# Attention scores from row slices of split features instead of stacked copies, and the mixed-feature loads in other slots of the weight region

## The chip, the cores and the metric

The kernel runs on one core of a Trainium2 chip. What counts is the device time of one execution in microseconds, as the median of several runs. All times are in microseconds unless ns stands beside them.

## What is computed

The reference is a backbone of two layers over 256 context tokens and 512 latent tokens, 1024 features wide, in float32. In each layer a modulated RMS norm and one input projection feed three mixers: differential attention (4 heads, each with two softmax components of 32 features), grouped-query attention (6 query heads, 2 key heads, 64 features) and a gated delta rule in both directions (6 heads, "GDN" below). Their outputs are joined, projected back and added; then follows a SwiGLU block. The last layer needs latent queries only. The two attention mixers, cut to what the change touches:

```
# differential attention
s = einsum('bqhcd,bkhcd->bhcqk', q, k) * scale        # two components c of 32 features each
p = softmax(s);  p = p[:, :, 0] - lam * p[:, :, 1]
o = einsum('bhqk,bkhe->bqhe', p, v)
# grouped-query attention
s = einsum('bqhgd,bkhd->bhgqk', q, k) * 64 ** -0.5
o = einsum('bhgqk,bkhd->bqhgd', softmax(s), v)
```

Latent queries read all 768 tokens, context queries the 256 context tokens.

## The kernel before, in words

Float32 products are made of float32r matmuls: a number x is split into hi, its rounding, and lo = x - hi, and a product becomes hi*hi + hi*lo + lo*hi (`mm3` and `split`, lines 222 to 233). Most of the time goes to the projections and the SwiGLU block, with features on the partitions and tokens on the free axis.

The change touches the mixers of each layer. `mixers` (line 972) runs a plan written out by hand (`PLAN`, line 38): its items `p` and `s` are the preparation and the twelve sequential steps of the GDN, `o` its output, `a` a piece of the attention. Program order and the given priorities go to a scheduler, which orders each engine's instructions by when it expects them to be ready; on the chip every engine then runs its own list in order.

The attention (`attention`, line 1268) goes over five pairs of heads in the order 2, 0, 3, 1, 4 (`HORD`). Pairs 0 and 1 are differential, 2 to 4 grouped-query. Within a pair it goes over query tiles of 128 tokens: four latent ones in both layers, two context ones in layer 0 besides. `ASTEP` says after which query tiles the next pair is prepared: `f` and `t` are the first and second part of `attn_prep` (line 1212), and `o` writes out the pair before.

`attn_prep` loads queries and keys with tokens on partitions, turns them on TensorE (tile `exp`) and splits them: `to_feat` (line 1092) leaves hi and lo with 128 features on the partitions, in slots of tag `f`. For a differential pair the 128 features are four components of 32 rows. For each component, `stack4` (line 1114) multiplies its 32 rows of hi and of lo by a constant 0/1 matrix `pick`, which is loaded by `pick_setup`, so that 128 rows hold (hi, hi, lo, lo) for queries and (hi, lo, hi, lo) for keys. The products stand in PSUM tile `stk` and are copied to SBUF tiles `qs` and `ks` (tag `t`): by VectorE where the columns are context, by ScalarE where they are latent. One matmul over 128 rows then gives all products of a score. `stack2` (line 1129) does the like for grouped-query pairs by copying halves of 64 partitions (`gqs`, `gks`); two matmuls give a score.

`scores` (line 1165) fills one PSUM tile `S` of two banks (768 columns as two halves of 384) for one softmax component. There are two such tiles, s0 and s1, taken in turn. `softmax` (line 1155) takes the maximum on VectorE (`nm`, line 1161) and the exponential on ScalarE (`P`, L182 in the rows). `attend` (line 1174) combines the two components of a differential head on VectorE, turns P on TensorE (`pt`, `PT`), and multiplies by V (`pv`). The PSUM tiles m0 and m1 are a ring (line 146) that `exp`, `stk`, `pt`, `pv` and `otr` share.

Last in the plan is `mixed` (line 958): it closes the GDN's memory and opens the weight region W of three raw slots, four hi slots and four lo slots (line 1422), loads seven of the eight mixed feature tiles from DRAM (`mx`, into the raw slots, on SyncE's queue) and splits them into `mhi` and `mlo`. The output projection `outproj` (line 1313) then loads the weights `w_o` through the same raw slots, on ScalarE's queue, and splits them (`whi`, `wlo`). Line 188 is the helper that issues every matmul of `mm`, 191 every transpose on TensorE, 185 every copy on ScalarE, 161 every two-operand VectorE or GpSimd operation, 182 every activation. In the rows TensorE is PE and its weight loads PEld, VectorE DVE, ScalarE ACT, GpSimd POOL. In a matmul's shape, as 32*128, the first number is the rows of the array that it uses.

Of the kernel before, what the change touches and what calls it, by code (L numbers as in the profile page):

```python
# [10 lines left out]
F32 = mybir.dt.float32  # L11
# [11 lines left out]
NT = TOK // 128  # L23
# [44 lines left out]
ATTN = (dict(t=10, f=4, p=4, q=3, v=2, d=2, w=2, g=4, u=1),  # L68
        dict(t=10, f=3, p=4, q=4, v=2, d=2, w=2, g=4, u=1))
# [25 lines left out]
class Net:  # L95
# [862 lines left out]
    def mixed(self, l, side, parts):  # L958
# [7 lines left out]
        for kt in self.early_k(l):  # L966
            x = self.W.slot("mx", F32, "raw")
            self.dma(x[:, t0:TOK], self.mixd[kt][:, t0:TOK])
            for a, n, _ in parts:
                self.split(self.at(self.mhi, kt, a, n), self.at(self.mlo, kt, a, n), x[:, a:a + n])  # L970
# [121 lines left out]
    def to_feat(self, src, t0, name):  # L1092

        hi, lo = (self.slot(name, F32R, tag="f") for _ in range(2))
# [7 lines left out]

    def pick_setup(self):

        self.pick = self.R.tiny("pick", [128, 4, 128], F32R)
        raw = self.slot("pickraw", tag="d")[:, :512]
        self.dma(raw, self.A["pick"])
        self.cp(self.pick.rearrange("p a b -> p (a b)"), raw)

    def parts_of(self, t0):  # L1110

        return ((t0, 2), (2, NT)) if t0 < 2 else ((2, NT),)

    def stack4(self, feat, c, kind, t0, name):

        x = self.slot(name, F32R, tag="t")
        r = slice(32 * c, 32 * c + 32)
        for a, b in self.parts_of(t0):
            ps = self.ring("stk")[:, :128 * (b - a)]
            w = slice(128 * a, 128 * b)  # L1120
            for hl in range(2):
                self.mm(ps, self.pick[r, 2 * kind + hl], feat[hl][r, w], hl == 0, hl == 1)
            if a < 2:
                self.v.tensor_copy(x[:, w], ps)
            else:
                self.cp(x[:, w], ps)
        return x

    def stack2(self, src, t0, name, k):


        out = [[self.slot(name, F32R, tag="g" if k else "t") for _ in range(2 if k else 1)] for _ in range(2)]
        for a, b in self.parts_of(t0):
            ps = self.ring("exp")
            w = slice(128 * a, 128 * b)
            for i in range(a, b):
                self.tr(ps[:, 128 * (i - a):128 * (i - a) + 128], src[:, i])
            for c in range(2):
                own, other = slice(64 * c, 64 * c + 64), slice(64 - 64 * c, 128 - 64 * c)
                p = ps[own, :128 * (b - a)]  # L1140
                hi, lo = out[c][0], out[c][-1]
                self.cp(hi[own, w], p)
                if k:
                    self.cp(hi[other, w], p)
                    self.sub(lo[own, w], p, hi[own, w].bitcast(F32))
                self.sub(lo[other, w], p, hi[own, w].bitcast(F32))
        return out
# [17 lines left out]
    def scores(self, pairs, qt, nk):  # L1165
        ps = self.big("S")
        halves = 2 if nk == 768 else 1
        w = nk // halves
        for hf in range(halves):
            for i, (qT, kT) in enumerate(pairs):  # L1170
                self.mm(ps[:, hf, :w], qT[:, 128 * qt:128 * qt + 128], kT[:, hf * w:hf * w + w], i == 0, i == len(pairs) - 1)
        return ps if nk == 768 else ps[:, 0, :nk]

    def attend(self, l, pair, O, qts):

        for qt in qts:
# [4 lines left out]
            for hd, (comps, V) in enumerate(pair):  # L1181
                Ps = [self.softmax(self.scores(pr, qt, nk), nk, Z[:, hd, ci:ci + 1]) for ci, pr in enumerate(comps)]
                P = Ps[0]
                if len(comps) == 2:
# [5 lines left out]
                for i, k0 in enumerate(range(0, nk, 384)):  # L1190
# [4 lines left out]
                    if i < EVD[l][len(comps) - 1]:  # L1195
# [7 lines left out]
            for kb in range(nkb):  # L1203
                for c in range(2):
                    self.mm(pv[64 * c:64 * c + 64, :128], pair[c][1][:, kb], PTs[c][:, 128 * kb:128 * kb + 128], kb == 0, kb == nkb - 1)
# [6 lines left out]
    def attn_prep(self, l, i):  # L1212


        t0 = 2 if l == DEPTH - 1 else 0
        if i < 2:
            q = self.load_tok(self.dqk[:, :, 128 * i:128 * i + 128], t0, "dq")
            k = self.load_tok(self.dqk[:, :, 256 + 128 * i:256 + 128 * i + 128], 0, "dk")
            q = self.to_feat(q, t0, "qT")
            yield  # L1220
            q = [self.stack4(q, c, 0, t0, "qs") for c in range(4)]
            k = self.to_feat(k, 0, "kT")
            comps = [[(q[c], self.stack4(k, c, 1, 0, "ks"))] for c in range(4)]
            vs = self.load_tok(self.dkv[:, :, 256 + 128 * i:256 + 128 * i + 128], 0, "vs", "v")
            yield [(comps[2 * c:2 * c + 2], vs[:, :, 64 * c:64 * c + 64]) for c in range(2)]
# [6 lines left out]
        q2 = self.stack2(q, t0, "gqs", False)  # L1232
        yield [([[(q2[c][0], k) for k in self.gks[c]]], self.gV[:, :, 64 * c:64 * c + 64]) for c in range(2)]
# [34 lines left out]
    def attention(self, l, parts):  # L1268

        order = HORD[l]  # L1270
        self.pick_setup()
# [302 lines left out]
def shape_consts():  # L1574
# [27 lines left out]
    pick = np.zeros((4, 32, 4, 4, 32), f)  # L1602
    for j, at in enumerate(((0, 1), (2, 3), (0, 2), (1, 3))):
# [62 lines left out]
```

## Time and profile before

| | us |
|---|---|
| median of 3 runs (lowest, highest) | 2182.35 (2180.88, 2187.04) |
| the profiled execution's own time | 2187.43 |
| its span, first to last instruction | 2185.6 |
| PE busy / VectorE busy / ScalarE busy in the span | 2020.9 / 1325.2 / 823.8 |
| mean granted TensorE clock, share of full speed | 0.943 |

Busy time of PE is counted from records in which matmuls overlap, so it is not PE at its peak. A stretch is named by microseconds from the start of the span, as 526 to 546. The mixers of layer 0 lie at about 345 to 627, those of layer 1 at about 1500 to 1741. The granted clock (PEclk) is 1.00 at 2.4 GHz and 0.50 at 1.2 GHz; a value between is a mean over both.

### The profile page before, as it was taken

To read this page: it belongs to the slowest core of one execution; us is meant where nothing else is said; L and a number is where in the kernel's file an instruction comes from. 1 tells how busy PE (TensorE), PEld (TensorE's weight loads), DVE (VectorE), ACT (ScalarE), POOL (GpSimd) and SP (SyncE) were. 2 spreads that over 40 slices of the span, in tenths; PEclk is the share of its full clock that TensorE was granted. 3 is DMA by queue.
4 is the path that set the end of the run, shared out by engine and by line. 5 is a ranking of instruction groups with operands and counts; after the bars stand their busy time and mean duration, and the time that the engine had idled before them with its cause. 6 is when DMAs were issued, how large, how long until landed. Compare 5 with 4: busy or idle time off the path is not lost. (4 is left out here: it accounts for less than half of the span.)

```text
span 2185.6 us, 36979 instructions
## 1 busy us (share of the span) xinstructions
PE 2020.9 (92%) x14786; PEld 1672.6 (77%) x14786; DVE 1325.2 (61%) x2223; ACT 823.8 (38%) x1609; POOL 525.0 (24%) x768
## 2 busy tenths in 40 slices
PE   7999877998889999999999989977899799999998
PEld 3788766776668888888888888865676598888887
DVE  6755774575845747565757457687767664443444
ACT  5433315464744321212122344423475653222223
POOL 2403579331014100000000350367323030000002
PEclk9999987698999999999999989987798999999999
DMA  8354434221062324343424411444212242222321
GB/s 296 121 176 132 156 109 113 47 73 35 26 227 78 116 87 154 110 131 102 155 91 140 134 56 48 133 127 125 51 47 60 86 165 77 100 85 92 106 98 61
DMA packets 167596, 236.46 MB, mean 108 GB/s; under 512 B 75328, under 2 KB 109248, under 8 KB 167424
## 3 DMA queue, kind: packets, MB, share of 16 engines
q10 hardware_dynamic: 46160, 144.92, 20.2%
q1 hardware_dynamic: 121264, 89.18, 13.4%
q8 instruction: 116, 1.90, 0.3%
q14 instruction: 56, 0.46, 0.1%
HBM read 198.00 MB, written 36.04 MB: 107 GB/s over the span
## 5 line engine op out<-in xcount | busy, mean ns | idle before, releaser
L185 ACT ACTIVATE whi<-raw 128x1024 fp32r<-128x1024 f32 (+4 forms) x246 | 220.7, 912 | 499.6 <-PE dps L188 207.3
L161 DVE TENSOR_TENSOR wlo<-raw,whi 128x1024 fp32r<-128x1024 f32 (+4 forms) x236 | 250.1, 1074 | 222.1 <-ACT whi L185 221.3
L188 PE MATMUL gu<-ahi,wlo 128*128 128x512 f32 x672 | 264.0, 393 | 1.1 <-DVE wlo L161 1.1
L188 PE MATMUL gu<-ahi,whi 128*128 128x512 f32 x672 | 263.6, 392 | 0.0
L188 PE MATMUL dps<-acth,whi 128*128 128x512 f32 (+1 forms) x560 | 186.6, 348 | 0.4 <-DVE h L179 0.2
L188 PE MATMUL dps<-acth,wlo 128*128 128x512 f32 (+1 forms) x560 | 185.7, 346 | 0.0
L188 PE MATMUL gu<-alo,whi 128*128 128x512 f32 x672 | 168.9, 392 | 0.0
L179 DVE SCALAR_TENSOR_TENSOR junk<-adaw,cb 128x1024 bf16<-128x1024 f32 x112 | 136.8, 1222 | 37.6 <-DMA adaw<-ada_t 36.6
L188 PEld LDWEIGHTS gu<-ahi,wlo 128*128 128x128 f32 x672 | 126.5, 188 | 28.3 <-DVE wlo L161 1.5
L188 PE MATMUL tps<-whi,ahi 128*128 128x512 f32 (+4 forms) x368 | 137.9, 379 | 11.1 <-ACT dq L185 7.2
L188 PEld LDWEIGHTS gu<-alo,whi 128*128 128x128 f32 x672 | 126.3, 188 | 27.6
L179 DVE SCALAR_TENSOR_TENSOR h<-dps,md,h 128x512 f32<-128x512 f32 (+1 forms) x128 | 80.6, 633 | 109.6 <-PE dps L188 109.3
L188 PEld LDWEIGHTS gu<-ahi,whi 128*128 128x128 f32 x672 | 126.5, 188 | 26.7
L188 PE MATMUL tps<-wlo,ahi 128*128 128x512 f32 (+4 forms) x368 | 138.3, 376 | 2.6 <-DVE wlo L161 2.4
L161 POOL TENSOR_TENSOR md<-md,adab 128x2 f32<-128x2 f32 x56 | 32.0, 572 | 439.5 <-DVE junk L179 439.5
L188 PE MATMUL tps<-whi,alo 128*128 128x512 f32 (+4 forms) x368 | 137.3, 373 | 0.0
L1161 DVE TENSOR_REDUCE nm<-S 128x1 f32<-128x768 f32 (+1 forms) x140 | 117.0, 844 | 32.6 <-PE S L188 31.4
L182 ACT ACTIVATE P<-S,nm 128x768 f32<-128x768 f32 (+1 forms) x140 | 114.0, 815 | 51.7 <-DVE nm L1161 46.1
L161 POOL TENSOR_TENSOR sqc<-sqc 128x256 f32<-128x256 f32 x35 | 35.4, 1012 | 397.8 <-ACT sqc L182 397.4
L188 PE MATMUL dps<-actl,whi 128*128 128x512 f32 (+1 forms) x560 | 124.3, 346 | 0.0
L188 PEld LDWEIGHTS dps<-acth,whi 128*128 128x128 f32 x560 | 105.4, 188 | 15.6 <-DVE h L179 0.4
L188 PEld LDWEIGHTS dps<-acth,wlo 128*128 128x128 f32 x560 | 105.7, 189 | 14.3
(295 smaller groups left out, 4629.0 us busy)
## 6 DMA issues: line engine op xcount, KB each, us to landing
raw<-w_u ACTq DMA_DIRECT2D x88, 512.0 KB
adaw<-ada_t ACTq DMA_DIRECT2D x56, 512.0 KB
adaw<-ada_p ACTq DMA_DIRECT2D x24, 512.0 KB
raw<-w_o ACTq DMA_DIRECT2D x24, 512.0 KB
raw<-w_d ACTq DMA_DIRECT2D x44, 256.0 KB
raw<-w_d ACTq DMA_DIRECT2D x32, 320.0 KB
adaq<-ada_q SPq DMA_DIRECT2D x16, 512.0 KB
raw<-w_t ACTq DMA_DIRECT2D x16, 512.0 KB
```

The source lines that it names most:

```text
L161: (eng or self.v).tensor_tensor(out=out, in0=a, in1=b, op=op)
L179: self.v.scalar_tensor_tensor(out=out, in0=a, scalar=sc, in1=b, op0=op0, op1=op1, **k)
L182: self.s.activation(out=out, in_=in_, func=func, **k)
L185: self.s.activation(out=out, in_=in_, func=AF.Copy, **k)
L188: self.t.matmul(out, lhsT, rhs, start=start, stop=stop)
L1161: self.v.tensor_reduce(out=nm, in_=pin, axis=AX.XY if nk == 768 else AX.X, op=ALU.max, negate=True)
```

## The change

Scores are made directly from row slices of the split features: three matmuls (hi*hi, hi*lo, lo*hi) of 32 rows for a differential component, of 64 rows for a grouped-query head. Two components, or two heads, are issued in turn into the two PSUM tiles s0 and s1. `pick_setup`, `stack4` and `stack2` are gone, and with them the tiles `pick`, `stk`, `qs`, `ks`; the numbers of slots change. Keys and queries of every pair now go through `to_feat`. The mixed features are loaded into the hi and lo slots of W in turn, where the raw slots were used.

```diff
-ATTN = (dict(t=10, f=4, p=4, q=3, v=2, d=2, w=2, g=4, u=1),
-        dict(t=10, f=3, p=4, q=4, v=2, d=2, w=2, g=4, u=1))
+ATTN = (dict(f=8, p=6, q=4, v=2, d=2, w=2, g=2, u=1),) * 2
...
-        for kt in self.early_k(l):
-            x = self.W.slot("mx", F32, "raw")
+        for i, kt in enumerate(self.early_k(l)):
+            x = self.W.slot("mx", F32, ("hi", "lo")[i % 2])
...
-    def scores(self, pairs, qt, nk):
-        ps = self.big("S")
+    def scores(self, feats, rows, qt, nk):
+
+        q, k = feats
+        ps = [self.big("S", j) for j in range(2)]
         halves = 2 if nk == 768 else 1
         w = nk // halves
         for hf in range(halves):
-            for i, (qT, kT) in enumerate(pairs):
-                self.mm(ps[:, hf, :w], qT[:, 128 * qt:128 * qt + 128], kT[:, hf * w:hf * w + w], i == 0, i == len(pairs) - 1)
-        return ps if nk == 768 else ps[:, 0, :nk]
+            for i, (a, b) in enumerate(((0, 0), (0, 1), (1, 0))):
+                for j, r in enumerate(rows):
+                    self.mm(ps[j][:, hf, :w], q[a][r, 128 * qt:128 * qt + 128], k[b][r, hf * w:hf * w + w], i == 0, i == 2)
+        return ps if nk == 768 else [x[:, 0, :nk] for x in ps]
...
-            for hd, (comps, V) in enumerate(pair):
-                Ps = [self.softmax(self.scores(pr, qt, nk), nk, Z[:, hd, ci:ci + 1]) for ci, pr in enumerate(comps)]
+            if not diff:
+                both = self.scores(feats, [r[0] for r in rows], qt, nk)
+            for hd in range(2):
+                ss = self.scores(feats, rows[hd], qt, nk) if diff else [both[hd]]
+                Ps = [self.softmax(x, nk, Z[:, hd, ci:ci + 1]) for ci, x in enumerate(ss)]
...
         if i < 2:
-            q = self.load_tok(self.dqk[:, :, 128 * i:128 * i + 128], t0, "dq")
-            k = self.load_tok(self.dqk[:, :, 256 + 128 * i:256 + 128 * i + 128], 0, "dk")
-            q = self.to_feat(q, t0, "qT")
+            q = self.to_feat(self.load_tok(self.dqk[:, :, 128 * i:128 * i + 128], t0, "dq"), t0, "qT")
             yield
-            q = [self.stack4(q, c, 0, t0, "qs") for c in range(4)]
-            k = self.to_feat(k, 0, "kT")
-            comps = [[(q[c], self.stack4(k, c, 1, 0, "ks"))] for c in range(4)]
+            k = self.to_feat(self.load_tok(self.dqk[:, :, 256 + 128 * i:256 + 128 * i + 128], 0, "dk"), 0, "kT")
...
+            rows = [[slice(64 * c + 32 * j, 64 * c + 32 * j + 32) for j in range(2)] for c in range(2)]
+            yield (q, k), rows, [vs[:, :, 64 * c:64 * c + 64] for c in range(2)]
             return
...
-            self.gks = self.stack2(self.load_tok(self.dkv[:, :, 0:128], 0, "gk"), 0, "gks", True)
+            self.gks = self.to_feat(self.load_tok(self.dkv[:, :, 0:128], 0, "gk"), 0, "gks", "g")
...
-        q2 = self.stack2(q, t0, "gqs", False)
-        yield [([[(q2[c][0], k) for k in self.gks[c]]], self.gV[:, :, 64 * c:64 * c + 64]) for c in range(2)]
+        q = self.to_feat(q, t0, "gqs")
+        yield (q, self.gks), [[slice(64 * c, 64 * c + 64)] for c in range(2)], [self.gV[:, :, 64 * c:64 * c + 64] for c in range(2)]
...
-        self.pick_setup()
```

## Rows read from the trace of the kernel before

**Rows 1.** The page: the span, and busy time, share and instructions of each engine.
```profile
span 2185.6 us, 36979 instructions
PE 2020.9 (92%) x14786; PEld 1672.6 (77%) x14786; DVE 1325.2 (61%) x2223; ACT 823.8 (38%) x1609; POOL 525.0 (24%) x768
```
**Rows 2.** Busy time by stretch, layer 0: length, engines with counts, PEclk, DMA share, GB/s.
```profile
403.00:427.00 24.00, 23.39 (x235) 16.24 (x236) 9.37 (x18) 12.00 (x26) 5.58 (x6) 0.51 0.14 31
...
526.00:546.00 20.00, 17.42 (x48) 9.72 (x47) 7.42 (x16) 7.79 (x15) 0.00 (x0) 0.59 0.00 0
546.00:571.00 25.00, 21.08 (x118) 14.04 (x117) 21.69 (x38) 16.79 (x39) 0.00 (x0) 0.78 0.04 16
```
**Rows 3.** Groups by line, 526 to 546: count | busy, mean ns | idle before, releasers.
```profile
L188 PE MATMUL stk<-kT,pick 32*128 32x256 f32 (+1 forms) x16 | 7.3, 600 | 1.4 <-ACT ks L185 0.9 <-DVE ks L1124 0.5
L188 PE MATMUL stk<-qT,pick 32*128 32x256 f32 (+1 forms) x16 | 5.3, 451 | 0.9 <-ACT qs L185 0.5 <-DVE qs L1124 0.2
...
L185 ACT ACTIVATE qs<-stk 128x512 fp32r<-128x512 f32 x4 | 2.4, 597 | 4.6 <-PE stk L188 4.6
...
L1124 DVE CAST ks<-stk 128x256 fp32r<-128x256 f32 x4 | 1.7, 425 | 3.7 <-PE stk L188 3.7
```
**Rows 4.** Busy time by stretch, layer 1: columns as in rows 2 (PE, PEld, DVE, ACT, POOL).
```profile
1540.00:1555.00 15.00, 10.20 (x135) 6.72 (x134) 14.51 (x30) 5.28 (x12) 9.37 (x11) 0.72 0.33 67
1555.00:1577.00 22.00, 21.45 (x264) 15.87 (x264) 10.63 (x23) 9.07 (x20) 5.59 (x7) 0.57 0.20 44
1577.00:1611.00 34.00, 31.05 (x643) 24.05 (x644) 24.21 (x45) 23.73 (x61) 7.46 (x9) 1.00 0.11 25
...
1652.00:1678.00 26.00, 24.28 (x284) 18.31 (x282) 17.43 (x37) 9.60 (x20) 10.35 (x11) 0.71 0.16 43
```
**Rows 5.** Groups by line and shape, 546 to 571: VectorE, then one of ScalarE.
```profile
L1161 DVE TENSOR_REDUCE nm<-S 128x1 f32<-128x768 f32 x14 | 13.2, 951 | 1.2 <-PE S L188 1.2
L179 DVE SCALAR_TENSOR_TENSOR P<-P,cR 128x768 f32<-128x768 f32 x7 | 7.1, 1018 | 0.2
...
L182 ACT ACTIVATE P<-S,nm 128x768 f32<-128x768 f32 x13 | 11.7, 901 | 7.4 <-DVE nm L1161 6.0 <-DVE P L179 0.8 <-DVE cR L1186 0.5
```
**Rows 6.** Groups by line and shape, 1711 to 1726 (a grouped-query pair, GDN done).
```profile
L1161 DVE TENSOR_REDUCE nm<-S 128x1 f32<-128x768 f32 x8 | 7.6, 955 | 2.7 <-PE S L188 2.7
L188 PE MATMUL S<-gks,gqs 128*128 128x384 f32 x32 | 7.4, 358 | 0.0
...
L188 PEld LDWEIGHTS S<-gks,gqs 128*128 128x128 f32 x30 | 5.0, 189 | 0.4 <-ACT P L182 0.4
```
**Rows 7.** ScalarE and its queue, then PE, in order of time at both layers' ends of the mixers.
```profile
611.32 0.94 ACT L185 ACTIVATE mhi<-mx 128x512 fp32r<-128x512 f32 x2 [2.25 <-DMA mx<-mixd]
...
1735.46 0.72 ACT L185 ACTIVATE mhi<-mx 128x256 fp32r<-128x256 f32 x2 [3.25 <-DMA mx<-mixd]
...
1740.80 0.34 ACTq L156 DMA_DIRECT2D raw<-w_o  x1
...
1747.72 1.06 ACT L185 ACTIVATE whi<-raw 128x1024 fp32r<-128x1024 f32 x1 [5.38 <-DMA raw<-w_o]
...
1748.83 0.58 PE L188 MATMUL ops<-mhi,whi 128*128 128x256 f32 x1 [7.65 <-ACT whi L185]
```
**Rows 8.** PE in order of time, merged: start, us to the last end, count.
```profile
426.04 1.65 PE L188 MATMUL S<-ks,qs 128*128 128x384 f32 x4
...
560.08 0.62 PE L188 MATMUL S<-ks,qs 128*128 128x384 f32 x2
...
588.81 0.94 PE L188 MATMUL S<-gks,gqs 128*128 128x384 f32 x4
...
1653.78 0.74 PE L188 MATMUL stk<-qT,pick 32*128 32x512 f32 x4
...
1670.55 1.64 PE L188 MATMUL stk<-kT,pick 32*128 32x256 f32 x4
```
**Rows 9.** VectorE's first group, 1577 to 1611: count | busy, mean ns | idle before, releasers.
```profile
L1161 DVE TENSOR_REDUCE nm<-S 128x1 f32<-128x768 f32 x14 | 13.0, 949 | 1.6 <-PE S L188 1.6
```

More of the change, by code (lines that the diff above doesn't have):

```diff
@@ L1090, in lam_prep, with to_feat @@
         self.ts(self.lam[:, l:l + 1], self.lam[:, l:l + 1], 1.0, -lam_init(l), ALU.mult, ALU.add, eng=self.g)
-    def to_feat(self, src, t0, name):
-        hi, lo = (self.slot(name, F32R, tag="f") for _ in range(2))
+    def to_feat(self, src, t0, name, tag="f"):
+        hi, lo = (self.slot(name, F32R, tag=tag) for _ in range(2))
         for a, b in ((t0, 2), (2, NT)) if t0 < 2 else ((2, NT),):
@@ L1101, in to_feat @@
         return hi, lo
[L1103 to L1147, printed above, removed]
     def load_tok(self, src, t0, name, tag="d"):
@@ L1169, in scores @@
         for hf in range(halves):
-            for i, (qT, kT) in enumerate(pairs):
-                self.mm(ps[:, hf, :w], qT[:, 128 * qt:128 * qt + 128], kT[:, hf * w:hf * w + w], i == 0, i == len(pairs) - 1)
-        return ps if nk == 768 else ps[:, 0, :nk]
+            for i, (a, b) in enumerate(((0, 0), (0, 1), (1, 0))):
+                for j, r in enumerate(rows):
+                    self.mm(ps[j][:, hf, :w], q[a][r, 128 * qt:128 * qt + 128], k[b][r, hf * w:hf * w + w], i == 0, i == 2)
+        return ps if nk == 768 else [x[:, 0, :nk] for x in ps]
     def attend(self, l, pair, O, qts):
+        feats, rows, vs = pair
+        diff = len(rows[0]) == 2
         for qt in qts:
@@ L1180, in attend @@
             Z = self.tiny("Z", [128, 2, 2], bufs=4)
-            for hd, (comps, V) in enumerate(pair):
-                Ps = [self.softmax(self.scores(pr, qt, nk), nk, Z[:, hd, ci:ci + 1]) for ci, pr in enumerate(comps)]
+            if not diff:
[3 more added lines that the diff above has]
+                Ps = [self.softmax(x, nk, Z[:, hd, ci:ci + 1]) for ci, x in enumerate(ss)]
                 P = Ps[0]
-                if len(comps) == 2:
+                if diff:
                     c = self.tiny("cR", [128, 1], bufs=4)
@@ L1194, in attend @@
                         self.tr(ps[:, k:k + 128], P[:, k0 + k:k0 + k + 128])
-                    if i < EVD[l][len(comps) - 1]:
+                    if i < EVD[l][diff]:
                         self.v.tensor_copy(PT[:, k0:k0 + n], ps[:, :n])
@@ L1204, in attend @@
                 for c in range(2):
-                    self.mm(pv[64 * c:64 * c + 64, :128], pair[c][1][:, kb], PTs[c][:, 128 * kb:128 * kb + 128], kb == 0, kb == nkb - 1)
+                    self.mm(pv[64 * c:64 * c + 64, :128], vs[c][:, kb], PTs[c][:, 128 * kb:128 * kb + 128], kb == 0, kb == nkb - 1)
             OT = self.R.tiny("OTs", [128, 128], bufs=2)
@@ L1600, in rope @@
         return np.ascontiguousarray(t.transpose(1, 0, 2, 3))
-    pick = np.zeros((4, 32, 4, 4, 32), f)
-    for j, at in enumerate(((0, 1), (2, 3), (0, 2), (1, 3))):
-        for b in at:
-            pick[:, :, j, b] = np.eye(32, dtype=f)
-    return {"ident": np.eye(128, dtype=f), "pick": pick.reshape(128, 512), "masks": masks.reshape(128, 768), "mloc": mloc,
+    return {"ident": np.eye(128, dtype=f), "masks": masks.reshape(128, 768), "mloc": mloc,
             "negm": np.concatenate([negm.reshape(128, 128), masks[:, 2:4].reshape(128, 256)], 1), "blk2": blk2,
```

1 line of the change is left out of this document (removed).

## The prediction, made blind

> **What bounds the kernel now.** I read the page first: PE is busy in 92% of the span, VectorE in 61%, ScalarE in 38% [rows 1]. That speaks for PE, but its records overlap, so the share says little of one stage. The change touches only the mixers, so next I read the busy times by stretch there. Where the `stk` products of a differential pair are made, no engine is full: in 526 to 546 PE issues 48 matmuls in 20 us at a clock of 0.59, VectorE is busy 7.4 us and ScalarE 7.8, and GpSimd does nothing [rows 2]. The groups of that stretch say why: 32 `stk` matmuls in pairs, and after each pair a copy (597 ns on ScalarE, 425 ns on VectorE), each copy idle before because of `stk`, the next matmul waiting for the copy [rows 3]. It is a chain through two ring buffers with one engine at work at a time. There are four such stretches, each with half of its time or more at the low clock: 403 to 427 and 526 to 546 in layer 0, 1555 to 1577 and 1652 to 1678 in layer 1 [rows 2, 4]. GDN work shares three of them.
>
> The attention proper is bound otherwise. In 546 to 571, with GDN done, VectorE is busy 21.7 of 25 us [rows 2]: 14 maxima at 0.95 and 7 combinations at 1.02 [rows 5]. That is 25/7 = 3.6 us for one head of two components. In a grouped-query pair alone, 1711 to 1726, there are 8 maxima in 15 us [rows 6], 3.75 us for a query tile of two heads. Last I read who waits at the end of the mixers: ScalarE stands 2.25 and 3.25 us for `mx`, in layer 1 then 5.38 us for `w_o`, and PE 7.65 us behind it [rows 7].
>
> **The change, part by part.** The sum goes against the profiled execution, 2187.4 us, which is 5.1 above the median of 2182.35.
>
> **Stacks.** They leave 112 matmuls and 56 copies less, two loads and copies of `pick`, and half or more of the copies to `gqs` and `gks`. Their busy time counts for nothing by itself; the chain does. In 526 to 546 nothing else was to be done, so of 20 us there stays the turning and splitting of the keys, some 4 us, which the two-step preparation with eight `f` slots can partly bring forward: 15 saved. In 403 to 427 a GDN preparation runs besides, which stays. But attention could run beside it as it does later; at the low clock, some 6 us a head, 24 us hold four heads, which are worth 4 x 3.6 = 14 later. In layer 1, VectorE is full until 1555 (14.5 of 15 us, a GDN inversion) [rows 4], so the first stretch gives less, 7; and the second holds the last GDN steps, which stay: 10. Sum 46. At most the four stretches, 92 us together, less 4 us each for the keys: 76. At least the one without GDN and a few us: 20. I stay in the middle, as three of four are shared.
>
> **Scores on PE.** Matmuls of S grow from 360 to 756, so what one costs decides. Four over 128 rows take 0.94 us at full clock, two take 0.62 [rows 8]: 0.16 for each, which is 384 columns at 2.4 GHz, and 0.30 for entry and drain. Two things must hold. Matmuls on different row groups must run side by side: four of 32 rows and 512 columns took 0.74 us, though 2048 columns one after another at 2.4 GHz are 0.85, so they do [rows 8]. And the weights of a row group must load beside a matmul on the same group: at half clock four `stk` of 32 rows, one component, 1536 columns, took 1.64 us, and four S over 128 rows with as many columns took 1.65 [rows 8]. So small row groups lose nothing there. The Trainium skill, TensorE: Matmul & The Clock Gate, Part 3, has a rule against the change: a weight load overlaps running matmuls only where the row group differs. By that rule each of the six steps of a call would carry its load; the trace disagrees, at half clock at least. So a call of six steps, two matmuls at once, takes 6 x 0.16 + 0.30 = 1.26 us. It replaces 2 x 0.62 = 1.24 for a differential head and 2 x 0.94 = 1.88 for a query tile of a grouped-query pair. Upper bound: a step of 0.16 + 0.19, the load's own duration [rows 6], and 2.4 us a call. I take 1.3, near the rows of the same shape.
>
> **Two PSUM tiles at once.** This is the new wait. A call needs s0 and s1. If the scheduler lets the first component start when its tile is free, a cycle is 1.3 + 0.95 (maximum) + 0.90 (exponential) [rows 5] = 3.15 us, below VectorE's 3.6: nothing lost. If both wait for the later exponential, it is one maximum more, 4.1 us: 0.5 a head. Queued behind that wait on PE are the `pt` and `pv` of the head before and the GDN's small matmuls. I take 0.35, nearer to lockstep since the matmuls are written in turn. With 32 latent heads (2 pairs, 2 heads, 4 tiles, 2 layers): 11 us, between 0 and 16. A grouped-query tile has the same cycle, 3.15 to 4.1, against 3.75: 24 such calls at 0.1 are 2 us, between -14 and +8. Context tiles are few and short: nothing. PE also enters and leaves another tile shape 70 times; that is in the 0.30 of each call. Two more P slots free exponentials earlier and cost nothing; VectorE hides it.
>
> **Mixed features.** In raw slots, `mx` went three at a time, and `w_o` could be issued only when they were split, at 1740.8, after which PE stood 7.65 us [rows 7]. In hi and lo slots all seven are issued together, and `w_o` goes ahead in the raw slots. ScalarE's waits for `mx` shrink too, with attention copies queued behind them. On SyncE's queue the loads of `h` stand behind `mx` and move forward with it. Then `mhi` is late next, and it needs the transfers anyway. I take 7 in layer 1 and 3 in layer 0, of 11 and 5 at most; at least 2 together, if transfers collide.
>
> Sum: -46 + 11 + 2 - 10 = -43. 2187.4 - 43 = 2144; on the scale of the median 2139, say 2140.
>
> **The rivals.** (a) The gaps belong to the GDN. Three stretches hold GDN steps in a sequence of their own, and attention moved into them pushes those back. For: in 1577 to 1611, where both run, 14 maxima, seven heads, need 34 us, 4.9 each [rows 4, 9]. Against: no engine is full in the gaps. Then 20 are saved, 7 at the end, and 13 are paid: 2187.4 - 14 - 5 = 2168. (b) The clock. Matmuls over 32 rows may not hold the full clock: all four stretches with `stk` show 0.51 to 0.71 [rows 2, 4]. Against: there PE also waits most of the time. A call then takes 6 x 0.32 + 0.37 = 2.3, in lockstep 5.1 a head, 1.5 x 32 = 48 paid: -56 + 48 + 2, 2176 on the median's scale. (c) **The slower side.** The loads of weights don't hide at full clock, where a load of 0.19 is longer than 384 columns (0.16); the row that shows them hidden is at half clock, where columns take 0.32. Place: every score call. Price: 2.4 us a call, in lockstep 5.2 a cycle, 1.6 x 32 + 1.45 x 24 = 86 against 56 gained: +30, 2212. It decides from a mean of 1.0 us lost a cycle, a call of some 1.9 us. (d) Better: tiles staggered, the gaps gone but for the keys: -70 - 12 - 5, about 2097. That the change doesn't do what it says is out: the stacks are gone from the code.
>
> **How the numbers follow.** Chances: the forecast 0.42, (a) 0.20, (b) 0.12, (c) 0.13, (d) 0.13. The range leaves out the better half of (d) and the worse half of (c): 2100 to 2200. A measurement can tell about 0.3% from no change, 2176 to 2189. Faster takes the forecast but for 0.02, (d), two thirds of (a) and half of (b): 0.40 + 0.13 + 0.13 + 0.06 = 0.72. Same takes 0.11: the 0.02, 0.05 of (a) and 0.04 of (b). Slower is (c) with what is left of (a) and (b), the GDN held up in earnest: 0.17.
>
> **What would show it.** Right: no `stk`; no stretch of some 20 us with all engines half idle ahead of a differential pair; S of 32*128 and 64\*128, six steps in about 1.3 us; a head in a lone differential pair every 3.6 to 4.1 us; PE's wait for `whi` after the mixers under 3 us. Wrong: the clock near 0.5 through differential pairs (b), steps of 0.3 us at full clock (c), the GDN steps later by what attention gains (a), or a head at over 4.6 us.

## The result and the profile after

The changed kernel is slower. Its median is 2246.95 us (2239.15 to 2259.36, 4 runs) beside 2184.69 (2180.88 to 2188.08, 4 runs) before: a ratio of 1.0291, 95% interval 1.0231 to 1.0350, or 62 us more. The forecast was 2140, in a range up to 2200.

The page of the execution after begins thus; each engine has its busy time, share and instructions. Its own time is 2259.36 us, the slowest of the four, so the stages below add up to 72 us against the profiled execution before, and not to 62.

```profile
span 2257.5 us, 37414 instructions
...
PE 2106.5 (93%) x15070; PEld 1753.1 (78%) x15070; DVE 1306.4 (58%) x2178; ACT 797.5 (35%) x1554; POOL 526.7 (23%) x768
```

PE has 284 matmuls more than before, and 86 us more of busy time [rows 1]. VectorE and ScalarE have less to do. The mean granted clock has gone from 0.943 to 0.915 in the profiled execution (0.918 to 0.928 in the other three). As a clock of 0.50 takes away half, the time at 1.2 GHz is 2 x (1 - clock) x span: 249 us before, 384 after.

Where the time went shows by stages. The first matmul of the output projection comes at 685.5 in layer 0, where it came at 621.9, and in layer 1 at 1823.1, where it came at 1748.8 [rows 7]: 64 us are lost up to the end of layer 0's mixers, 11 more up to the end of layer 1's, where the mixed features give some back. Layer 0 before, then after:

```profile
621.95 0.50 PE L188 MATMUL ops<-mhi,whi 128*128 128x512 f32 x1 [0.69 <-ACT whi L185]
...
685.49 0.80 PE L187 MATMUL ops<-mhi,whi 128*128 128x512 f32 x1
```

Next the busy times by stretch after the change, for layer 0. The first three are the gaps ahead of the pairs 0, 3 and 1; the fourth holds the latent query tiles of the differential pair 1, when the GDN is done, and the fifth the rest of that pair and the last grouped-query pair.

```profile
core 0: us, PE busy (x) PEld busy (x) DVE busy (x) ACT busy (x) POOL busy (x), PEclk, DMA share, GB/s
383.00:411.00 28.00, 23.77 (x336) 17.84 (x334) 15.24 (x33) 9.83 (x25) 11.88 (x13) 0.89 0.28 68
481.00:506.00 25.00, 24.25 (x330) 18.20 (x329) 6.40 (x16) 10.53 (x29) 4.88 (x6) 0.61 0.10 25
544.00:571.00 27.00, 23.41 (x378) 18.29 (x376) 20.50 (x48) 10.36 (x26) 13.01 (x13) 1.00 0.28 75
571.00:625.00 54.00, 51.66 (x204) 39.95 (x204) 28.72 (x50) 22.88 (x52) 0.28 (x1) 0.51 0.03 11
630.00:672.00 42.00, 38.65 (x244) 28.06 (x244) 23.44 (x51) 22.71 (x59) 2.27 (x1) 0.80 0.31 113
```

The fourth row is the one to read: 54 us for eight heads of two components, 6.8 us a head, PE busy in 51.7 of them, and the clock at 0.51. Before, a head took 3.6 us in such a stretch: VectorE filled it (21.7 of 25 us) at a clock of 0.78 [rows 2]. Now the bound is PE, at half speed. The groups of that stretch, by form:

```profile
L187 PE MATMUL S<-kT,qT 32*128 32x384 f32 x96 | 30.1, 541 | 3.0 <-ACT P L181 2.3 <-ACT kT L184 0.7
...
L1114 DVE TENSOR_REDUCE nm<-S 128x1 f32<-128x768 f32 x16 | 15.0, 955 | 10.9 <-PE S L187 10.9
L181 ACT ACTIVATE P<-S,nm 128x768 f32<-128x768 f32 x16 | 14.4, 900 | 17.8 <-DVE nm L1114 17.8
L190 PE MATMUL pt<-ident,P 128*128 128x128 f32 x42 | 11.3, 431 | 0.0
```

The maxima wait 10.9 us for scores, where 14 of them waited 1.2 us before [rows 5]. The same stretch on PE in order of time (start, us to the last end, count):

```profile
584.97 2.29 PE L187 MATMUL S<-kT,qT 32*128 32x384 f32 x6
587.18 1.97 PE L187 MATMUL pv<-PT,vs 128*64 128x128 f32 x14
589.08 2.29 PE L187 MATMUL S<-kT,qT 32*128 32x384 f32 x6
```

Six matmuls of one component stand alone, 6 x 0.32 = 1.92 us at low clock and 0.37 for entry and drain. The forecast had 1.26 us for both components together. Where one component's six matmuls stand together like this, nothing runs side by side.

At the end of the mixers the loads of `w_o` now go ahead of the last splits:

```profile
1788.27 0.37 ACTq L155 DMA_DIRECT2D raw<-w_o  x1
...
1793.78 0.72 ACT L184 ACTIVATE mhi<-mx 128x256 fp32r<-128x256 f32 x2 [0.48 <-DMA mx<-mixd]
1796.40 1.07 ACT L184 ACTIVATE whi<-raw 128x1024 fp32r<-128x1024 f32 x1
...
1823.14 0.39 PE L187 MATMUL ops<-mhi,whi 128*128 128x256 f32 x1
```

The first weights are split 27 us ahead of their use; PE's wait of 7.65 us for them [rows 7] is gone.

### The profile page after: what moved, and what is told of

It is laid out like the page before. It is cut to its first block, busy times and chain, and to the rows that moved or that the text cites. A ratio compares the mean times of both kernels' runs of the same rounds, so it can differ in the third digit from the quotient of the medians.

```text
span 2257.5 us, 37414 instructions
## 1 busy us (share of the span) xinstructions
PE 2106.5 (93%) x15070; PEld 1753.1 (78%) x15070; DVE 1306.4 (58%) x2178; ACT 797.5 (35%) x1554; POOL 526.7 (23%) x768
## 5 line engine op out<-in xcount | busy, mean ns | idle before, releaser
L190 PE MATMUL pt<-ident,P 128*128 128x128 f32 x520 | 110.6, 343 | 13.5 <-ACT P L181 8.1
```

What stands on the lines that cost most here:

```text
L190: self.t.transpose(out, in_, self.ident)
```

## The experiments

Three theories stood at first. **T1**: scores over few rows leave PE at 1.2 GHz, and everything in the stretch pays. **T2**: order; a call needs both PSUM tiles and its components run one after the other. **T3**: the GDN is pushed back by the attention moved into its gaps.

### One part at a time

The first four split the change. `mx_only` is the kernel before with one edit:

```diff
-        for kt in self.early_k(l):
-            x = self.W.slot("mx", F32, "raw")
+        for i, kt in enumerate(self.early_k(l)):
+            x = self.W.slot("mx", F32, ("hi", "lo")[i % 2])
```

> The kernel before with the mixed-feature loads alone moved to the hi and lo slots; scores and stacks as before. Theories for the 62 us that the whole change lost: T1, the clock (PE stays at 1.2 GHz wherever score matmuls use few rows, and the whole attention stretch runs at half speed); T2, order (a call needs both PSUM tiles, its six steps of the two components run one component after the other, and the softmax waits for them); T3, the GDN steps are pushed back by attention that moved into their gaps. None of the three touches the mixed features: all expect 2172 to 2179 us here, 6 to 12 us below before (7 of them in layer 1, where PE waited 7.65 us for w_o's weights). If it comes out within 2 us of before, the earlier output projection seen after the change came from the later attention and not from the slots.

Measured: 2173.72, ratio 0.9935 (0.9921 to 0.9949), 15 us less. The prediction gave it 10. In layer 1 the first load of `w_o` is issued at 1679.34 instead of 1740.80 [rows 7], its split is at 1688.86 instead of 1747.72, and PE starts at 1733.08 instead of 1748.83, without a wait:

```profile
1679.34 0.33 ACTq L156 DMA_DIRECT2D raw<-w_o  x1
...
1688.86 1.06 ACT L185 ACTIVATE whi<-raw 128x1024 fp32r<-128x1024 f32 x1
...
1733.08 0.38 PE L188 MATMUL ops<-mhi,whi 128*128 128x256 f32 x1
```

`gqa_only` puts only the grouped-query half of the diff into the kernel before, `diff_only` only the differential half.

> Grouped-query scores alone in the new form (three matmuls over 64 rows per half, two heads in turn), differential pairs with their stacks as before, mixed features in raw slots as before. T1: 64 rows may hold the clock better than 32; if the clock fell with 64 rows too (as the trace after the change shows at 644 to 661) 20 to 30 us slower than before, about 2210. T2: a call of six steps for two heads in lockstep, cycle 4.1 us against 3.75 before: 24 x 0.35 = 8 us, less the shorter preparation, 2185 to 2195. T3: within 5 us of before, since the grouped-query preparation made no gap.

> Differential scores alone in the new form (three matmuls over 32 rows per half and component, no stk products), grouped-query pairs stacked as before, mixed features in raw slots. T1: the differential pairs carry nearly all of the loss: about 2245 (after the change without the 10 us that the mixed features gave back), and the lone pair 1 of layer 0 again at a clock near 0.5. T2: 32 heads at 5.1 instead of 3.6 us, +48, less the stacks' 20 to 40: 2195 to 2215, with the clock at 0.9 or more in the lone pair. T3: 2170 to 2190.

Measured: 2233.31, ratio 1.0203 (1.0177 to 1.0229), 44 us more, for the grouped-query part; 2243.14, ratio 1.0251 (1.0238 to 1.0264), 54 us more, for the differential one. T1's 2245 for the latter holds, and so does its lone pair, by the busy times of that stretch: 

```profile
563.00:620.00 57.00, 54.37 (x219) 42.44 (x219) 29.66 (x54) 23.86 (x56) 0.00 (x0) 0.50 0.02 7
```

But "nearly all of the loss" does not: the grouped-query part alone costs nearly as much, more than any theory said. And its loss is not the clock alone: at a mean clock of 0.931 it has 309 us at 1.2 GHz, 60 more than before, which cost at most 30 of the 53 us between the two profiled executions. Where the rest went is open. The parts don't add up either: 44 + 54 - 15 is 83, and the change lost 62.

`nostk` takes the stacks away and pays nothing for it: it has as many score matmuls as before, over the unstacked hi features, so the scores leave out the lo parts and mix the components (cut to the matmuls; the mixed features stay in the raw slots).

```diff
-            for i, (a, b) in enumerate(((0, 0), (0, 1), (1, 0))):
-                for j, r in enumerate(rows):
-                    self.mm(ps[j][:, hf, :w], q[a][r, 128 * qt:128 * qt + 128], k[b][r, hf * w:hf * w + w], i == 0, i == 2)
+            for j in range(2):
+                for i in range(n):
+                    self.mm(ps[j][:, hf, :w], q[0][:, 128 * qt:128 * qt + 128], k[i][:, hf * w:hf * w + w], i == 0, i == n - 1)
```

> The kernel before without its stacked copies and with nothing paid for it: preparation and slots as after the change, mixed features in the raw slots, and the scores as many full-row matmuls as before (one per half for a differential component, two for a grouped-query head) over the unstacked hi features, so the products leave out the lo parts and mix the components. This measures the term of 46 us that the prediction gave the stacks, by itself. By the prediction 2188 - 46 = 2142, with 2112 to 2168 as its bounds. If the gaps ahead of the differential pairs belong to the GDN (T3): 2165 to 2185.

Measured: 2129.51, ratio 0.9720 (0.9687 to 0.9754), 63 us less. So the stacks were worth more than the 46 of the prediction. T3 (2165 to 2185) falls: the GDN is not pushed back, its last `scan` on PE starts at 497.4 instead of 507.1 in layer 0 and at 1630.5 instead of 1670.3 in layer 1. But the gaps don't close. Ahead of pair 0 no score matmul runs for 34 us, where it was 40, and ahead of pair 1 for 30, where it was 27; that second gap is now filled by the GDN and the pair before (before, then `nostk`, columns as in rows 2):

```profile
513.00:540.00 27.00, 21.61 (x108) 12.77 (x107) 10.61 (x28) 7.84 (x20) 2.61 (x2) 0.81 0.10 29
...
482.00:512.00 30.00, 26.36 (x371) 19.55 (x370) 20.83 (x49) 11.79 (x28) 12.46 (x12) 1.00 0.27 75
```

Some of the gain comes before any differential pair: the first score matmul starts at 331.2 instead of 345.8, as the preparation ahead of it, without `pick` and the copies to `gqs` and `gks`, is shorter. With this and the 15 of the mixed features, the scores of the change must have cost 62 + 63 + 15 = 140 us, if parts add; the prediction gave them 13.

### Rows and clock

`rows128` lets each score matmul of the change run over all rows, `rows64` those of a differential component over the 64 of its head:

```diff
-                    self.mm(ps[j][:, hf, :w], q[a][r, 128 * qt:128 * qt + 128], k[b][r, hf * w:hf * w + w], i == 0, i == 2)
+                    self.mm(ps[j][:, hf, :w], q[a][:, 128 * qt:128 * qt + 128], k[b][:, hf * w:hf * w + w], i == 0, i == 2)
```

```diff
                 for j, r in enumerate(rows):
+                    r = slice(64 * (r.start // 64), 64 * (r.start // 64) + 64)
```

> The changed kernel with every score matmul over all 128 rows (same count, same columns, same PSUM tiles; the sums then run over all four components or both heads, so the scores are other numbers, and no two of them can run side by side). T1: the clock goes back to 0.9 or more through the lone differential pair of layer 0, and although PE now has 12 steps one after another (12 x 0.16 = 1.9 us a call at full clock) the kernel is no slower than the change, 2200 to 2245. T2: serial steps cost more than before whatever the clock: 12 x 0.16 + 0.3 = 2.2 us a call against 1.3 to 2 side by side: 2260 or above. T3 makes no difference to the change, 2247.

> The change with the differential scores over the 64 rows of a head in place of the 32 of a component (same count, both components on the same rows, so no two side by side; the sums run over both components, so the scores are other numbers); grouped-query scores unchanged at 64 rows. T1 with rows in use at one time: 64 rows one after another use the array as two times 32 side by side do, the lone differential pair stays near 0.5 and pays 12 x 0.32 us a call: 2270 to 2320. T1 with each matmul's own rows: the clock comes half the way, 2210 to 2250.

`rows128` took 2162.07, ratio 0.9884 (0.9866 to 0.9902): faster than before, and 89 us below the change by the two ratios, with as many matmuls and none of them side by side. That is T1's side, beyond its range; T2 said 2260 or more. The same two stages as above in its busy times, and two groups of the first:

```profile
528.00:571.00 43.00, 38.42 (x276) 32.55 (x276) 31.67 (x64) 27.22 (x69) 0.00 (x0) 0.96 0.03 10
576.00:601.00 25.00, 22.11 (x179) 18.67 (x178) 16.16 (x32) 16.18 (x37) 2.27 (x1) 1.00 0.44 164
...
L187 PE MATMUL S<-kT,qT 128*128 128x384 f32 x96 | 21.6, 365 | 4.2 <-ACT P L181 3.3 <-ACT kT L184 0.7
...
L190 PE MATMUL pt<-ident,P 128*128 128x128 f32 x52 | 8.4, 289 | 0.1
```

The mean clock is 0.964: 156 us at 1.2 GHz, 228 fewer than in the change. At half speed these can cost at most 114; 89 came back, with the changes of shape gone too. If parts add, scores over all rows still cost 63 + 15 - 27 = 51 us more than stacked ones.

`rows64` took 2239.29, ratio 1.0227 (1.0183 to 1.0271). Its stages:

```profile
557.00:616.00 59.00, 56.72 (x236) 45.20 (x238) 29.93 (x54) 24.76 (x59) 0.00 (x0) 0.57 0.03 11
625.00:651.00 26.00, 24.15 (x178) 17.07 (x175) 16.49 (x32) 16.64 (x39) 2.27 (x1) 1.00 0.52 189
```

The total lies in the range of each matmul's own rows (2210 to 2250), but the lone differential pair at 0.57 is not half the way up; it is near the 0.5 of rows in use, whose total (2270 to 2320) missed. The second row is what neither had: the grouped-query pair, whose code is that of the change, ran at 1.00, with 26 us from its first score to its last (624.7 to 650.3) instead of 33 (638.9 to 671.5) in a stretch at 0.80. The clock depends on more than the present matmuls.

`row_series` measures that by itself: a block on PE in one execution of the kernel before, ahead of layer 1's attention, with nothing else, no change of shape within a part, no waits.

```diff
+SERIES = ((200, 128, 1), (300, 64, 1), (200, 128, 1), (300, 32, 1), (300, 64, 1), (300, 64, 2), (300, 32, 2), (300, 32, 4), (200, 128, 1))
...
+            for count, n, side in SERIES:
+                for _ in range(count):
+                    for i, r in enumerate(at[n][:side]):
+                        with self.tc.issue_after(last) if last is not None else ExitStack():
+                            last = self.t.matmul(ps[i % 2][:, i // 2, :384], qT[r, 256:384], kT[r, 0:384], start=True, stop=True).ins
```

> The kernel before with 3900 matmuls of 384 columns put in as one block ahead of layer 1's attention, back to back on PE with nothing between them and their results unread: 200 over 128 rows; 300 over 64; 200 over 128; 300 over 32; 300 over 64; 300 pairs of 64 side by side; 300 pairs of 32; 300 sets of four times 32; 200 over 128. PE waits for nothing and each part has one shape, so whatever the clock does here it does for the rows. T1 by rows in use at one time: 128, 2 x 64 and 4 x 32 at 1.00 and 0.16 us a step; 32 falls to 0.50 and 0.32 us; 64 and 2 x 32 alike. T1 by each matmul's own rows: 2 x 64 like 64, 2 x 32 and 4 x 32 like 32, all low. If the low clock comes from changes of shape and from waits: 1.00 in every part. Side by side holds if a pair or a set of four takes a step of 0.16 or 0.32 us.

The busy times of the block's own matmuls, a stretch inside each part from the second to the eighth (the counts in brackets are matmuls):

```profile
core 0: us, PE busy (x) PEld busy (x), PEclk, DMA share, GB/s
1560.00:1600.00 40.00, 40.00 (x232) 40.00 (x231) 1.00 0.00 1
1604.00:1637.00 33.00, 33.00 (x193) 33.00 (x192) 1.00 0.00 0
1645.00:1730.00 85.00, 85.00 (x268) 85.00 (x267) 0.50 0.00 0
1735.00:1825.00 90.00, 90.00 (x283) 90.00 (x283) 0.50 0.00 0
1835.00:1880.00 45.00, 45.00 (x523) 45.00 (x521) 1.00 0.01 1
1885.00:1930.00 45.00, 45.00 (x522) 45.00 (x521) 1.00 0.01 1
1935.00:1984.00 49.00, 49.00 (x1140) 49.00 (x1136) 1.00 0.01 3
```

Read downwards: 64 rows after 128 stay at 1.00 (40 us / 232 = 0.17 a step); 128; 32 rows fall to 0.50 (0.32 a step) though PE is busy all the time; **the same 64 rows after that stay at 0.50**; pairs of 64 side by side go back to 1.00; pairs of 32 side by side, entered at 1.00, stay there; so do four times 32. A pair or a set of four takes 0.17 us, so side by side costs nothing. This is T1 by rows in use at one time, but with a memory that nobody had expected: with 64 rows in use the clock stayed at whichever level it was found. The rival that shape changes and waits alone make the clock low falls, as neither is here.

With `rows128` that accounts for the differential pairs of the change: a component's six matmuls alone have 32 rows in use, and 32 rows brought the clock down. A grouped-query head alone has 64, and 64 did not bring it back. `rows64` and `rows128` fit, in this order:

```profile
550.00:560.00 10.00, 7.55 (x44) 4.88 (x44) 5.67 (x16) 3.56 (x8) 4.57 (x4) 1.00 0.17 48
560.00:610.00 50.00, 48.10 (x175) 38.22 (x175) 25.59 (x43) 20.65 (x46) 0.00 (x0) 0.51 0.02 8
...
530.00:540.00 10.00, 7.63 (x35) 6.49 (x34) 6.17 (x11) 4.82 (x11) 0.00 (x0) 0.83 0.00 0
540.00:571.00 31.00, 29.28 (x238) 24.88 (x236) 24.81 (x53) 22.08 (x58) 0.00 (x0) 1.00 0.04 14
```

Both enter the lone pair with PE busy in some 7.6 of 10 us, and in both the clock falls; over 64 rows it stays low with PE busy 48 of 50 us, over 128 it comes back. What made it fall there, a wait or a change of shape, is not told by a block without them. Pairs of 32 entered at the low clock were not tried.

### Order

`paired` chains the twelve matmuls of a call in their written order, so that components always run side by side.

```diff
+                    with self.tc.issue_after(last) if last is not None else ExitStack():
+                        last = self.t.matmul(ps[j][:, hf, :w], q[a][r, 128 * qt:128 * qt + 128], k[b][r, hf * w:hf * w + w],
+                                             start=i == 0, stop=i == 2).ins
```

> The change with one thing added: the twelve matmuls of a score call are chained in the order in which they are written, so that the two components or heads always run step by step beside each other, never one component's six alone. T1 in the form that the clock goes by the rows in use at one time: two grouped-query matmuls of 64 rows fill the array and the clock of the grouped-query stretches goes up, two of 32 rows fill half and the lone differential pair stays near 0.5; in all 2205 to 2230. T1 in the form that each matmul's own rows count: no stretch changes its clock, 2240 to 2260. T2 (order alone): calls of 1.3 to 2.3 us in place of up to 3.3, 56 x 0.5 = 28 us less, 2215 to 2225, whatever the clock.

Measured: 2238.91, ratio 1.0218 (1.0150 to 1.0286), which overlaps the change's interval: undecided on the time, outside the ranges of all three forms, and the mean clock is 0.915 again. The lone differential pair and the grouped-query pair after it, by busy times, and two groups of the first:

```profile
553.00:605.00 52.00, 43.53 (x275) 31.40 (x273) 31.67 (x64) 27.13 (x69) 0.00 (x0) 0.74 0.04 12
610.00:645.00 35.00, 28.55 (x199) 20.37 (x198) 20.31 (x38) 19.64 (x47) 2.27 (x1) 0.75 0.45 157
```

```profile
L1129 PE MATMUL S<-kT,qT 32*128 32x384 f32 x96 | 17.8, 439 | 7.4 <-ACT P L181 6.8 <-DVE kT L160 0.4
L1114 DVE TENSOR_REDUCE nm<-S 128x1 f32<-128x768 f32 x16 | 14.6, 951 | 5.0 <-PE S L1129 5.0
```

The scores' busy time falls from 30.1 to 17.8 and the clock is at 0.74 instead of 0.51, but PE now waits 6.8 us for exponentials that free the second tile. That is the lockstep of the prediction, and the stretch is hardly shorter, 52 us beside 54. Nor did the clock of the grouped-query pair rise, as rows in use had it (0.75 beside 0.80 in the change).

`filler` tries to hold the clock with more work, a matmul over all rows ahead of each half, overwritten at once; `filler_diff` does so in differential calls alone, `filler_paired` with the chain as well.

```diff
+            for x in ps:
+                self.mm(x[:, hf, :w], q[0][:, 128 * qt:128 * qt + 128], k[0][:, hf * w:hf * w + w])
```

> The change with work added and none taken away: ahead of the three products of each half and PSUM tile one more matmul over all 128 rows (hi queries by hi keys), which the first product overwrites, so that the full result stays. A score call has 16 matmuls in place of 12, 4 x 0.16 us more at full clock. T1 (the clock falls because the score matmuls keep few rows of the array in use): the extra full-row matmuls hold the clock up and the kernel gets faster by doing more: 2165 to 2215, with the lone differential pair of layer 0 above 0.75. T2 or any cause on PE's own columns: 56 calls x 0.64 to 1.3 us more, 2280 to 2320.

> The same full-row matmul ahead of each half, in the differential calls alone; grouped-query calls as in the change, 64 rows. T1: where the differential pairs hold the clock, the grouped-query pairs enter at 2.4 GHz; the run with 64 rows in both kinds showed a lone grouped-query pair at 1.00 throughout, so they may stay there: within 15 us of the version with the extra matmul in both kinds, 2165 to 2225. If 64 rows lose the clock by themselves, 2205 to 2235. T2: 2270 or above.

> The extra full-row matmuls of both kinds, and the matmuls of a call chained in the order in which they are written, so that both components or heads run side by side after them. T1: clock as with the extra matmuls alone; side by side a call has 4 + 6 steps of 0.16 us in place of up to 16, so 10 to 30 us below that version if the scheduler does not lose more by waiting for both PSUM tiles: 2150 to 2200. If the wait for both tiles is what counts (T2), no better than that version, or slower by up to 20.

Measured: 2390.64 (ratio 1.0949, 1.0902 to 1.0996), 2345.20 (1.0712, 1.0678 to 1.0746) and 2256.52 (1.0313, 1.0278 to 1.0348). T1 as I had stated it missed all three; T2 met only the 2270 or above of `filler_diff`. In the first, PE in order of time and the clock of the lone pair:

```profile
591.74 7.56 PE L187 MATMUL S<-kT,qT 128*128 128x384 f32 x16 [2.07 <-ACT P L181]
```

```profile
587.00:648.00 61.00, 58.93 (x186) 37.75 (x186) 22.21 (x37) 16.95 (x37) 0.00 (x0) 0.53 0.01 4
```

Sixteen matmuls of 384 columns at low clock are 16 x 0.32 = 5.1 us; they took 7.56. There are eight changes of shape, between 128 and 32 rows (the one into the transposes behind them counted), so each costs some 0.3 us. One full matmul among three of 32 rows did not raise the clock. So changes of shape have a price of their own on PE, beside the clock's. With the components side by side there are half as many changes, and 134 us come back; side by side itself and a mean clock of 0.936 instead of 0.902 are among them, so what part the changes have is not shown.

### Versions with the full result

`masked` runs the scores over all rows with queries that are zero outside their component, eight masks of queries for a differential pair on GpSimd; `masked_va` puts the masks on VectorE (hi) and ScalarE (lo). The line of `masked`, where `MENG` gives GpSimd:

```diff
+                self.ts(y[:, 128 * t0:TOK], x[:, 128 * t0:TOK].bitcast(F32), self.own[n][:, c:c + 1], None, ALU.mult, eng=MENG(self, c))
```

> A version that computes the full result with scores over all 128 rows and without stacks: queries are multiplied by 0/1 columns on GpSimd, so that a component's (or head's) queries are zero outside its own rows, and meet the unmasked keys of all rows; three full-row matmuls per half and component, mixed features in the hi and lo slots as after the change. T1: the clock as with all 128 rows and wrong products (0.964), 2162 plus what the 8 or 4 masks of a pair cost on GpSimd: 2160 to 2185. T2: slower than the change, since no two matmuls run side by side: above 2250.

> The masked version again (scores over all 128 rows, queries zero outside their component's rows, full result), with the masks of hi on VectorE and those of lo on ScalarE in place of GpSimd, which took 2.0 us a mask and up to 16 us in a row for a differential pair, and had held up 49 maxima by 55 us. T1: the mean clock at 0.955 or more as in the runs over all rows, and the time near the 2162 of the run with wrong products plus 56 masks of 0.4 to 0.8 us on two engines, partly on the path: 2165 to 2190. If VectorE and ScalarE are what bounds the attention, the masks cost there what they saved on GpSimd: 2195 to 2215.

Measured: 2208.53 (ratio 1.0079, 1.0049 to 1.0108) and 2190.45 (1.0007, 0.9995 to 1.0019), at clocks of 0.955 and 0.958. T1 holds for the clock; the time of the first missed; its masks take long on GpSimd (first row; then those of `masked_va`):

```profile
L177 POOL TENSOR_SCALAR mq<-qT,own 128x768 fp32r<-128x768 f32 x8 | 17.5, 2205 | 0.2 <-ACT qT L188 0.2
...
L188 ACT ACTIVATE mq<-qT,own 128x768 fp32r<-128x768 f32 x8 | 6.8, 925 | 0.4 <-DVE qT L164 0.4
...
L177 DVE TENSOR_SCALAR mq<-qT,own 128x768 fp32r<-128x768 f32 x8 | 5.1, 691 | 0.0
```

On VectorE such a mask takes 0.69 us and on ScalarE 0.93; that took off 18 us, and the kernel equals the one before.

`dmastack` keeps the stacks and the scores of before, with the mixed features in the new slots, but copies 32-row blocks of the split features by DMA, on SyncE's queue. `dmastack2` issues every second block of a differential stack from ScalarE's queue; `dmastack_d2` leaves the grouped-query stacks to copies as before. The line of these two:

```diff
+        for b in range(4):
+            (self.nc.scalar if b % 2 else self.nc.sync).dma_start(out=x[32 * b:32 * b + 32, 128 * t0:TOK].bitcast(F32), in_=feat[b % 2 if kind else b // 2][32 * c:32 * c + 32, 128 * t0:TOK].bitcast(F32))
```

> A version in which the stacks stay and no compute engine makes them: queries and keys of every pair are turned and split as in the change, and 32-row (64-row for grouped-query) blocks of hi and lo are copied into the stacked tiles by DMAs on SyncE's queue, 32 for a differential pair; scores as before, one full-row matmul per half or two; mixed features in the hi and lo slots. If the price of the scores is the clock and the stacks' chain was worth the 62 us that the run without stacks gave (T1): 2115 to 2150, with a mean clock of 0.95 or more. If the loads behind those DMAs on SyncE's queue, or their landing, take the chain's place: 2160 to 2200.

> Stacks by DMA again, with every second block of a differential stack issued from ScalarE's queue instead of SyncE's: with one queue the 16 blocks of the queries took 10.5 us and the 16 of the keys 10.1 us to issue, one after another, as long as the stk chain that they replaced (mean clock 0.940, no faster than before). If the issue was what held it, each group now takes some 5 us and 15 to 40 us come back over four preparations: 2145 to 2172, clock 0.945 or more. If the landing of the transfers or the loads behind them hold it, 2180 to 2190.

> The same for the differential pairs alone; grouped-query queries and keys are stacked by copies as before, without DMAs, which takes the 4 DMAs of each grouped-query pair and the 8 of its keys off SyncE's queue. If the issue on the queues is what counts: 2140 to 2172, within 10 us of the version with both. If ScalarE's copies of the grouped-query stacks are on the path: 5 to 15 us above that version.

Measured: 2186.82 (ratio 0.9985, 0.9971 to 0.9998), 2173.18 (0.9944, 0.9924 to 0.9963) and **2150.42 (0.9837, 0.9814 to 0.9859)**. The first had put one chain in another's place, as SyncE's queue in `dmastack` shows ahead of pair 1:

```profile
523.04 10.53 SPq L151 DMA_DIRECT2D qs<-qT  x16
...
538.78 10.06 SPq L151 DMA_DIRECT2D ks<-kT  x16
```

In `dmastack_d2` half of the same stacks' blocks are on that queue, in 7.5 and 5.3 us:

```profile
509.45 7.46 SPq L1118 DMA_DIRECT2D qs<-qT  x8
...
525.28 5.28 SPq L1118 DMA_DIRECT2D ks<-kT  x8
```

The last version beats both kernels, by 34 us and by some 97. Of the 34, 15 are the mixed features' (`mx_only`); beside that run, by the ratios, `dmastack` is some 11 us slower and `dmastack2` the same. Against expectation the grouped-query blocks cost more as DMAs than as copies: 23 us between the last two versions. Which of the loads behind them was late was not followed up.

## Why the prediction was wrong

**The step that failed is "Scores on PE", and with it rival (b).** The prediction priced a call by the full clock, 6 x 0.16 + 0.30. The call's steps were right: 0.17 us at 1.00, side by side, loads hidden. But the clock doesn't stay at 1.00, and the scores cost 140 us, if parts add, in place of 13. Rival (b) named this cause, with a chance of 0.12 and a price of 48 us, and its signs came: 0.51 through the lone differential pair, and 6.8 us a head. It was rated low because PE also waited in the stretches with `stk` [rows 2, 4]; the block of single shapes shows that 32 rows are enough, without any wait. Three things are missing from its price. It charged the differential heads only, and the grouped-query calls alone cost 44 us, though at most 30 by the clock. It charged the scores only, where transposes (431 ns against 289 in `rows128`) and everything else on PE in those stretches run at half speed too. And it let components run side by side, where the change's trace shows six matmuls alone. What is left with the clock up, 51 us in `rows128`, goes with 396 score matmuls more and the wait for two PSUM tiles, which no run divides; for the change itself no run held the clock up, so how its 140 us divide between clock, shape changes and order is not settled beyond the 89 us between `rows128` and the change.

**Stacks.** 46 us between bounds of 20 and 76: measured 63. The size was within the bounds, and ahead of pair 1 the stretch with no engine full is gone, but the gain did not come as it was summed: the pauses of the scores ahead of the differential pairs stayed in layer 0, and the scores start 15 us earlier ahead of any differential pair, where the prediction gave `pick` and the grouped-query copies nothing. How the 63 divide is not shown. Rival (a), attention that pushes the GDN back, falls with the same run, where the GDN ends earlier. In the change itself the last `scan` of layer 0 comes at 562.3 instead of 507.1, and gaps of 25 to 28 us still stand ahead of three pairs (the first three rows of its stages), with GDN steps and products of the pair before in them; that they are work pushed there by slow scores is read from the trace alone.

**Rival (c), loads that don't hide at full clock**, falls: in the block, weight loads are busy the whole time and a step is 0.17 us, same row group or not. The Trainium skill, TensorE: Matmul & The Clock Gate, Part 3, says that a load overlaps running matmuls only where the row group differs; 232 matmuls on the same 64 rows in 40 us disagree. The prediction's own rows had it for 128 rows at full clock: four S stand 0.16 apart, with loads of 0.19 on the same rows [rows 6, 8]. The Trainium skill, TensorE: Matmul & The Clock Gate, Part 1, has the clock follow how busy PE has been; here PE was busy 85 of 85 us over 32 rows, at 0.50, so busy time alone doesn't tell the clock.

**Two PSUM tiles at once.** The wait exists (6.8 us in the lone pair of `paired`). In the change it hardly shows, 2.3 us of PE waiting for exponentials in the fourth stretch, where components run alone; by the two traces the one cost stands in the other's place. "PE also enters and leaves another tile shape" was counted inside the 0.30 of a call; `filler` shows some 0.3 us for each change at low clock.

**Mixed features.** 10 us predicted, 15 measured (11 to 17 by the interval), mostly in layer 1 as forecast: the first product of the projection comes 1.6 us earlier in layer 0 (620.34) and 15.7 in layer 1, so some 14 were gained between. The mechanism was the predicted one; the gain in layer 0 was over-sized and that in layer 1 under-sized. In the sum of rival (d) there is a slip of a few us (the terms give 2100 or 2095, not 2097); no chance hangs on it.

## What to carry to other kernels

Price a matmul that uses few rows of the array at both clock levels, and charge the low one to everything else that PE does in the stretch. Before swapping a copy chain for more, smaller matmuls, measure the two terms apart: one run without the copies and one with the new matmul count over full rows told 63 and, with the mixed features taken off, 51 us here, where the sum alone told nothing. Copies can also leave the engines as DMAs, but count their issue, 0.65 us each or more on a queue here.

## What the runs showed that was not expected

The clock kept the level that it had: 64 rows ran 40 us at 1.00 after 128 rows and 90 us at 0.50 after 32 rows, the same instructions. Four matmuls of 32 rows side by side took 0.17 us, as long as one of 128, and kept 1.00. Rows that hold zeros kept the clock too: with three quarters of a differential pair's queries (half of a grouped-query pair's) masked to zero the mean clock was 0.955. A mask of 128 x 768 took 2.2 us on GpSimd, over three times VectorE's 0.69.
